# A new order of the steps of both mixing stages, its buffer table, and VectorE or GpSimd for 29 more instructions a layer

## The chip, the cores and the metric

The kernel runs on one core of a Trainium2 chip, as one launch. The metric is the device time of that launch in microseconds (us). Three runs of the kernel before took 1262.16, 1263.69 and 1265.23 us, the median being 1263.69.

The engines are named as in the profile: PE is TensorE (matrix products into PSUM), DVE is VectorE, ACT is ScalarE, POOL is GpSimd, and SP is the queue that issues the DMAs. Each engine works through a queue of its own in order; an instruction that waits for another engine holds up all that stands behind it in its queue.

## The reference

Two layers of a hybrid decoder trunk for 512 positions of width 1024: a mixing stage of three kinds of heads side by side, and an MLP with a squared ReLU, then a last norm. All in float32.

```python
for l in range(DEPTH):                              # DEPTH = 2
    h = rms_norm(x, norm_mix_g[l])
    proj = h @ w_in[l]                              # 1024 -> 3*384 + 3*256 + 1408
    p_att, p_conv, p_rwkv = jnp.split(proj, [3 * ATT_W, 3 * ATT_W + 3 * CONV_W], axis=-1)
    q, k, v = jnp.split(p_att, 3, axis=-1)
    ...
    o_att = diff_attention(q, k, v, lam, subln_g[l], lambda_init)    # 6 heads, causal
    b_gate, c_gate, u = jnp.split(p_conv, 3, axis=-1)
    o_conv = short_conv(b_gate, c_gate, u, conv_w[l])                # 3 taps
    o_rwkv = rwkv7_time_mix(p_rwkv, ...)                             # 6 heads, a recurrence over the positions
    mixed = jnp.concatenate([o_att, o_conv, o_rwkv], axis=-1)
    x = x + mixed @ w_out[l]
    h = rms_norm(x, norm_mlp_g[l])
    x = x + jnp.square(jax.nn.relu(h @ w_mlp_up[l])) @ w_mlp_down[l]
return rms_norm(x, final_norm_g)
```

## The kernel before

**Tiling.** x is held transposed, as eight tiles x 0 to x 7 of 128 channels by 512 positions. A projection is cut into groups of 128 output columns. To keep float32 accuracy each operand is a sum of two parts, a rounded one and its rest: for the activations ahim and alom (written by ACT at L431 and by DVE at L432), for the weights whi (the cast, ACT, L679) and wlo (the rest raw - whi, L691, on DVE or POOL). A weight group comes in two halves of 128x512 (named 0 and 4 by their first input tile), into three buffers each for raw, whi and wlo. One group is 24 products of 128x512, three for each input tile (ahim with whi, alom with whi, ahim with wlo), all through the helper of line L296, into one PSUM bank pj. Its evacuation, a DVE operation that multiplies with the norm's reciprocal root rsm (pk, pg, pr at L804, kf at L1259, vf at L1286), frees the bank.

**The mixing stage.** It has 26 groups of input projection, the differential attention of three head pairs, the short convolution, RWKV-7 for three head pairs, 8 output groups in two cuts (po, added to x at L732), and the first three groups of the MLP's up-projection (up). While PE works through the products of the groups, the small work of the heads is put between them: Gram products pg of RWKV (L296, from ar and bk, which DVE and POOL make at L942 to L945 from kkn, bb and k), transposes pk, pb, pa (L301), the scores sc of the attention, the masked row maximum (L1318), the exponentials (ACT, L1325), the weighted difference pp of the two softmaxes (L1332), its transposes ptt (L301) with their copies pT (ACT, L1341). RWKV's 64x64 triangular inverse starts with a chain of small POOL operations (tt and xb, L1150 and L1152). The norms' sums of squares run over the tiles: accm (L447) before the mixing stage, accf (L761) before the MLP; ones products pssm and pssf add them up over the channels, and a power on POOL (L377) and broadcast products prb make the reciprocal root.

**The order.** Nothing in the mixing stage is scheduled by the framework. The work is a set of generators, one a kind (m the products of the groups, w the casts, x and y the rests on DVE and on POOL, d the loads, e and q the entry's two parts, R, r, A, B and so on the heads' work), and a string of letters a layer, ORDER, says which generator emits its next instruction:

```python
for run in order.split():
    for _ in range(int(run[1:] or 1)):
        if next(work[run[0]], True) is None:
```

So each engine's queue has the order of that string. A second table, SLOTS, says which buffer of a tag each new tile takes (PSUM banks among them); a tile waits for the readers of the buffer's last tile. LO has a letter for each weight half: x puts its rest on DVE, y on POOL. SIDE has 29 letters a layer, read by `side` for: seven of the sums accf, and the RWKV operations k2 (L934), bb (L938), bk (L943), plo (L1008), nm (L1136), ee (L1176) of three pairs, and two each of the convolution's cz and cy (L1240, L1247); before, all 29 are on POOL.

The MLP that follows (groups up and dn, through L296, L352 and L353) is scheduled by the framework, from the state in which the mixing stage leaves the engines and banks.

Of the kernel before, what the change touches and what calls it, by code (L numbers as in the profile page):

```python
# [49 lines left out]
SIDE = ("yyyyyyyyyyyyyyyyyyyyyyyyyyyyy",  # L50
        "yyyyyyyyyyyyyyyyyyyyyyyyyyyyy")
# [4 lines left out]
LO = ("xxyyxxxxyxxyxyxyxyxyyxxxxyyxyyxxxyxyxyyyxxyxyyxxxxxyxxyyyxxyxyyyxxyxxyxxyyx",  # L56
      "xyxyyxxxxxyxxxxxxxxxxyxxyyyyyyxxyxxxxyyyyyyyxxxxyxxyyxyxyyxxyyxyxyyxyxxxxx")

ORDER = (
# [58 lines left out]
SLOTS = (  # L118
         "cp/rk 010 "
         "cp/ro 010 "  # L120
         "cp/rr 01 "
         "cp/rsx 01201201 "
         "cp/ry 010 "
         "cp/ys 010 "
# [158 lines left out]
def tile_trunk(ctx: ExitStack, tc: tile.TileContext, xT, wts, prm_d, cst_d, lora_d, gup_d, lam_d, fin_d, out):  # L283
# [85 lines left out]
    def root_steps(y, x, n, pad, add=None):  # L369
# [8 lines left out]
        for _ in range(pad):  # L378
            yield True
# [1241 lines left out]
```

## Time and profile before

| | |
|---|---|
| runs, median | 1263.69 us |
| the profiled execution, its own time | 1263.21 us |
| its span, first to last instruction | 1261.3 us |
| granted PE clock, share of full speed | 0.998 |
| mixing stages (layer 0, layer 1), about | 0 to 305, 632 to 925 us |

The profile has one execution. Its page gives the busy time of each engine; the list of waits gives, for an engine and an operation, by what it was held up: microseconds in total, times, longest. In the timeline a row has start, duration, engine, line, operation, result and operands by name, and in brackets the idle time before it with the operation that ended it. Groups of instructions have count, then busy time and mean duration in ns, then the idle time before them.

### The profile page before, as it was taken

How to read it: one execution, taken by the hardware profiler on the slowest of the kernel's cores; microseconds unless marked ns; L12 is line 12 of the kernel's file. 1: busy time of each engine (PE TensorE's matmuls, PEld its weight loads, DVE VectorE, ACT ScalarE, POOL GpSimd, SP SyncE). 2: the span in 40 equal slices, each digit the busy share in tenths (PEclk: the TensorE clock that was granted, in tenths of full speed). 3: DMA queues.
4: the chain of work that ended last, by engine and by line, in shares of the span. 5: the costliest groups of instructions: out<-in, count | busy, mean ns of one | idle time of the engine just before them, and what ended most of it. 6: DMA issues, size and time to landing. Idle time of an engine off the chain costs nothing.

```text
span 1261.3 us, 25029 instructions
## 1 busy us (share of the span) xinstructions
PE 1240.0 (98%) x9493; PEld 1049.8 (83%) x9493; DVE 889.3 (71%) x1728; ACT 695.4 (55%) x1474; POOL 359.4 (28%) x464
## 2 busy tenths in 40 slices
PE   9999999999999999999999999999999999999997
PEld 6777878787789898989877787888887989898987
DVE  6787777857967676765667777778598666666654
ACT  6675755646745454544475656564565545454553
POOL 1344627243200101010224355453431011111110
PEclk9999999999999999999999999999999999999999
DMA  6523323142333332321235333331424333333122
GB/s 213 159 85 94 109 94 101 52 140 78 106 121 101 101 101 101 101 86 50 77 101 146 98 102 109 98 97 60 134 93 134 96 106 100 102 101 101 60 76 76
DMA packets 84696, 127.92 MB, mean 101 GB/s; under 512 B 21472, under 2 KB 25568, under 8 KB 84576
## 3 DMA queue, kind: packets, MB, share of 16 engines
q1 hardware_dynamic: 83856, 125.77, 31.4%
q8 instruction: 75, 1.23, 0.4%
q10 hardware_dynamic: 720, 0.55, 0.1%
q14 instruction: 45, 0.37, 0.1%
HBM read 117.11 MB, written 9.18 MB: 100 GB/s over the span
## 4 chain that ended last, share of the span: by engine, by line
PE 70%; DVE 4%; issue 2%; ACT 2%; POOL 0%; POOLq 0%; ACTq 0%; DVEq 0%
PE dn L296 22%; PE pj L296 11%; PE pa L296 11%; PE pb L296 6%; PE po L296 4%; PE up L296 4%; PE dnF L296 3%; PE pc L296 3%; PE sc L296 1%; DVE wlo L353 1%; PE ptt L301 1%; PE pg L296 1%; DVE blo L1455 0%; DVE x L1531 0%; PE pyy L296 0%
## 5 line engine op out<-in xcount | busy, mean ns | idle before, releaser
L1399 POOL TENSOR_TENSOR ml<-m,mh 128x512 fp32r<-128x512 f32 x64 | 93.4, 1461 | 506.3 <-ACT mh L1398 488.3
L352 ACT CAST whi<-raw 128x512 fp32r<-128x512 f32 x142 | 88.0, 620 | 174.0 <-PE dn L296 156.8
L296 PE MATMUL dn<-mh,whi 128*128 128x512 f32 x448 | 175.4, 391 | 2.2 <-DVE x L1531 2.2
L296 PE MATMUL dn<-ml,whi 128*128 128x512 f32 x448 | 174.7, 390 | 0.0
L296 PE MATMUL dn<-mh,wlo 128*128 128x512 f32 x448 | 174.7, 390 | 0.0
L296 PE MATMUL pj<-ahim,whi 128*128 128x512 f32 x392 | 157.7, 402 | 4.4 <-DVE vf L1286 1.7
L296 PE MATMUL pj<-ahim,wlo 128*128 128x512 f32 x392 | 158.3, 404 | 0.0
L296 PE MATMUL pj<-alom,whi 128*128 128x512 f32 x392 | 158.2, 403 | 0.0
L679 ACT CAST whi<-raw 128x512 fp32r<-128x512 f32 x142 | 87.7, 619 | 100.1 <-PE pj L296 41.4
L1531 DVE TENSOR_TENSOR x<-dn,x 128x512 f32<-128x512 f32 x112 | 76.9, 687 | 77.4 <-PE dn L296 77.4
L691 POOL TENSOR_TENSOR wlo<-raw,whi 128x512 fp32r<-128x512 f32 x62 | 81.3, 1311 | 166.1 <-ACT whi L679 153.0
L353 DVE TENSOR_TENSOR wlo<-raw,whi 128x512 fp32r<-128x512 f32 x142 | 115.3, 812 | 11.3 <-ACT whi L352 11.2
L1470 DVE TENSOR_TENSOR slo_p<-s,shi_p 128x512 fp32r<-128x512 f32 x96 | 70.9, 741 | 63.4 <-ACT shi_p L1469 60.8
L296 PEld LDWEIGHTS dn<-mh,whi 128*128 128x128 f32 x448 | 84.0, 188 | 21.8 <-ACT whi L352 2.6
L296 PEld LDWEIGHTS dn<-mh,wlo 128*128 128x128 f32 x448 | 84.1, 188 | 17.9
L296 PEld LDWEIGHTS dn<-ml,whi 128*128 128x128 f32 x448 | 84.1, 188 | 16.5
L296 PEld LDWEIGHTS pj<-ahim,whi 128*128 128x128 f32 x392 | 73.9, 188 | 19.8 <-issue 1.7
L1469 ACT CAST shi_p<-s 128x512 fp32r<-128x512 f32 x96 | 59.2, 618 | 49.7 <-PE pa L296 38.1
L296 PEld LDWEIGHTS pj<-ahim,wlo 128*128 128x128 f32 x392 | 73.8, 188 | 14.3 <-issue 0.9
L296 PEld LDWEIGHTS pj<-alom,whi 128*128 128x128 f32 x392 | 73.9, 188 | 14.0 <-issue 0.5
L296 PE MATMUL pa<-tlo,shi_p 128*128 128x256 f32 x288 | 81.4, 282 | 0.0
L296 PE MATMUL pa<-thi,shi_p 128*128 128x256 f32 x288 | 81.2, 282 | 0.0
(406 smaller groups left out, 3247.5 us busy)
## 6 DMA issues: line engine op xcount, KB each, us to landing
raw<-wts SPq DMA_DIRECT2D x389, 256.0 KB, 2.6
qs<-dqhi SPq DMA_DIRECT2D x24, 128.0 KB, 3.2
ks<-dkhi SPq DMA_DIRECT2D x24, 128.0 KB, 3.8
x<-xT SPq DMA_DIRECT2D x8, 256.0 KB, 4.5
dqhi<-qhi SPq DMA_DIRECT2D x6, 256.0 KB, 3.3
dqlo<-qlo SPq DMA_DIRECT2D x6, 256.0 KB, 3.1
dkhi<-khi SPq DMA_DIRECT2D x6, 256.0 KB, 2.6
dklo<-klo SPq DMA_DIRECT2D x6, 256.0 KB, 3.1
```

What stands on the lines that cost most here:

```text
L296: ins = nc.tensor.matmul(*a, **k)
L301: ins = nc.tensor.transpose(*a, **k)
L352: act.copy(hi[:, :n], raw[:, :n])
L353: (pool if a and lean[0] else dve).tensor_tensor(lo[:, :n], raw[:, :n], hi[:, :n].bitcast(F32), ALU.subtract)
L679: yield act.copy(hi[:, k0:k1], raw[:, k0:k1])
L691: yield eng.tensor_tensor(lo[:, k0:k1], raw[:, k0:k1], hi[:, k0:k1].bitcast(F32), ALU.subtract)
L1399: pool.tensor_tensor(lo, m, hi.bitcast(F32), ALU.subtract)
L1469: act.copy(hi, src)
L1470: dve.tensor_tensor(lo, src, hi.bitcast(F32), ALU.subtract)
L1531: dve.tensor_tensor(x[j], pt, x[j], ALU.add)
```

## The change

The four tables are written anew: ORDER and SLOTS of both layers, LO, and SIDE. `root_steps` loses its empty steps, which emitted nothing. The program has the same 11870 instructions as before and two more ACT_TABLE_LOAD. 39 weight rests go from DVE to POOL; 42 instructions go from POOL to DVE, 15 of them weight rests, 27 by SIDE (layer 0: accf 1, 3, 7, k2 of pair 2, bb of pair 0, all bk, all nm, cz 1, cy 0; layer 1: accf 1, 2, 3, 4, 5, 7, k2 of pair 0, bk of pairs 0 and 2, plo of pair 0, ee of pair 1, cz 0). On PE 1261 of 6780 rows move; of 577 pieces of small work between the groups' products 218 stand elsewhere, most by one or two products. Of SP's 537 transfers 42 move, by at most three places.

```diff
-SIDE = ("yyyyyyyyyyyyyyyyyyyyyyyyyyyyy",
-        "yyyyyyyyyyyyyyyyyyyyyyyyyyyyy")
+SIDE = ("xyxyyyxyyxxyyxxxyyyxxxyyyyxxy",
+        "xxxxxyxxyyyyyxyxxyyyyyyxyxyyy")
...
-LO = ("xxyyxxxxyxxyxyxyxyxyyxxxxyyxyyxxxyxyxyyyxxyxyyxxxxxyxxyyyxxyxyyyxxyxxyxxyyx",
-      "xyxyyxxxxxyxxxxxxxxxxyxxyyyyyyxxyxxxxyyyyyyyxxxxyxxyyxyxyyxxyyxyxyyxyxxxxx")
+LO = ("xxxxxxyxyxyyyxxxyyyyyxyxxyyyyyyyxxxxyyyyxyyyyxxyxxxyyyyyyyyyyxxxxyyxxxxxxy",
+      "xyxyyxxxyyxxyyxyxxyxyyxyyyyyyxxxyyyxyxyyyyyyyxxxxxyyyyyyyyyyxyxyxxxxyyxxyy")
 ORDER = (
-         "g d10 e w e m w x m w m x m2 x m q m2 w m x e m w e m x m w d m3 x d e m3 d2 e q m3 d e q m3 d q e d q d q d q w d w d x d w x d x d q m d "
...
-    def root_steps(y, x, n, pad, add=None):
+    def root_steps(y, x, n, add=None):
...
         yield pool.tensor_tensor(y, xx, mhalf.to_broadcast([P, n]), ALU.pow)
-        for _ in range(pad):
-            yield True
-
```

What the strings do is seen in the queues. Rows give the source line, which is 14 to 17 less after the change, the operation, result and operands (the number behind the last underscore counts tiles), and the shape.

DVE near the start of layer 0, at 10 to 17 us, before:

```order
L432 SCALAR_TENSOR_TENSOR alom0_3_191<-x3_72,prm0_66,ahim0_3_190 128x512
L447 TENSOR_TENSOR accm0_149<-accm0_149,sqm0_2_198 128x512
L447 TENSOR_TENSOR accm0_149<-accm0_149,sqm0_3_204 128x512
L691 TENSOR_TENSOR wlo24_s_111<-raw24_4_166,whi24_s_110 128x512
L691 TENSOR_TENSOR wlo18_s_113<-raw18_4_172,whi18_s_112 128x512
L691 TENSOR_TENSOR wlo15_s_115<-raw15_4_180,whi15_s_114 128x512
L447 TENSOR_TENSOR accm0_149<-accm0_149,sqm0_4_222 128x512
L432 SCALAR_TENSOR_TENSOR alom0_4_229<-x4_73,prm0_66,ahim0_4_228 128x512
L432 SCALAR_TENSOR_TENSOR alom0_5_241<-x5_74,prm0_66,ahim0_5_240 128x512
```

and after:

```order
L430 TENSOR_TENSOR accm0_149<-accm0_149,sqm0_2_195 128x512
L430 TENSOR_TENSOR accm0_149<-accm0_149,sqm0_3_201 128x512
L415 SCALAR_TENSOR_TENSOR alom0_3_199<-x3_72,prm0_66,ahim0_3_198 128x512
L674 TENSOR_TENSOR wlo24_s_111<-raw24_4_170,whi24_s_110 128x512
L674 TENSOR_TENSOR wlo18_s_113<-raw18_4_172,whi18_s_112 128x512
L415 SCALAR_TENSOR_TENSOR alom0_4_227<-x4_73,prm0_66,ahim0_4_226 128x512
L430 TENSOR_TENSOR accm0_149<-accm0_149,sqm0_4_230 128x512
L674 TENSOR_TENSOR wlo15_s_115<-raw15_4_180,whi15_s_114 128x512
L415 SCALAR_TENSOR_TENSOR alom0_5_241<-x5_74,prm0_66,ahim0_5_240 128x512
```

alom 3 went behind two sums; alom 4 went ahead of a sum and of the rest of group 15. On ACT ahim 4 went ahead of the square sqm 4 in the same way, and on PE the sum product pssm went seven products back.

ACT in layer 0 at 47 to 57 us (L926 and L927 the exponentials of the decay, L850 the sigmoid of the pair's a), before:

```order
L926 ACT_TABLE_LOAD
L926 ACTIVATE dx0_0_573<-lw0_0_451 128x8x64
L927 ACTIVATE di0_0_574<-lw0_0_451 128x512
L679 CAST whi25_4_605<-raw25_4_514 128x512
L932 ACTIVATE t10_0_609<-av0_0_499,drv0_101,prm0_66 128x512
L936 ACTIVATE kkn0_0_621<-zk0_0_465,prm0_66 128x512
L679 CAST whi1_0_629<-raw1_0_562 128x512
L1292 COPY v0_0_637<-pvt0_0_638 128x512
L1325 ACTIVATE pp0_0_0_0_0_674,s0q0_0_650<-pp0_0_0_0_0_674,mx0_0_0_0_0_675 128x128
```

and after:

```order
L909 ACT_TABLE_LOAD
L909 ACTIVATE dx0_0_571<-lw0_0_448 128x8x64
L662 CAST whi25_0_576<-raw25_0_477 128x512
L910 ACTIVATE di0_0_572<-lw0_0_448 128x512
L915 ACTIVATE t10_0_600<-av0_0_499,drv0_101,prm0_66 128x512
L662 CAST whi25_4_602<-raw25_4_514 128x512
L919 ACTIVATE kkn0_0_612<-zk0_0_467,prm0_66 128x512
L833 ACT_TABLE_LOAD
L833 ACTIVATE av0_2_627<-pa0_2_624,prm0_66 128x512
L662 CAST whi1_0_634<-raw1_0_540 128x512
L1275 COPY v0_0_638<-pvt0_0_639 128x512
L1308 ACT_TABLE_LOAD
```

The sigmoid av0_2, which stood with those of the other pairs, now stands between the exponentials, and two table loads come with it. Its products pa0_2 on PE moved with it, from the first groups to the end of group 6. On DVE at this place bb, ar, vf and bk of pair 0 now follow each other, where bb and bk were on POOL.

PE at the end of input group 20 in layer 0, at 129 to 132 us, before:

```order
L301 MATMUL pb_0_1_1790<-cst_77,bk0_1_1634 128x128 x4
L296 MATMUL pj0_20_1694<-ahim0_5_240,wlo20_4_1581 128x512
L296 MATMUL pj0_20_1694<-ahim0_6_252,whi20_4_1575 128x512
L296 MATMUL pj0_20_1694<-alom0_6_253,whi20_4_1575 128x512
L296 MATMUL pj0_20_1694<-ahim0_6_252,wlo20_4_1581 128x512
L296 MATMUL pj0_20_1694<-ahim0_7_261,whi20_4_1575 128x512
L301 MATMUL pa_0_1_1811<-cst_77,ar0_1_1633 128x128 x4
L296 MATMUL pj0_20_1694<-alom0_7_262,whi20_4_1575 128x512
L296 MATMUL pj0_20_1694<-ahim0_7_261,wlo20_4_1581 128x512
L296 MATMUL sc0_1_0_0_0_1829<-ks0_1_0_1383,qs0_1_0_1348 128x128
L296 MATMUL sc0_1_0_0_1_1831<-ks0_1_0_1383,qs0_1_0_1348 128x128
L296 MATMUL pj0_17_1842<-ahim0_0_130,whi17_0_1656 128x512
```

and after:

```order
L282 MATMUL pj0_20_1721<-ahim0_6_252,wlo20_4_1578 128x512
L282 MATMUL pj0_20_1721<-ahim0_7_269,whi20_4_1576 128x512
L282 MATMUL pj0_20_1721<-alom0_7_270,whi20_4_1576 128x512
L282 MATMUL pj0_20_1721<-ahim0_7_269,wlo20_4_1578 128x512
L282 MATMUL sc0_1_0_0_0_1811<-ks0_1_0_1383,qs0_1_0_1346 128x128
L282 MATMUL sc0_1_0_0_1_1813<-ks0_1_0_1383,qs0_1_0_1346 128x128
L287 MATMUL pb_0_1_1817<-cst_77,bk0_1_1637 128x128 x4
L287 MATMUL pa_0_1_1835<-cst_77,ar0_1_1636 128x128 x4
L282 MATMUL pj0_17_1844<-ahim0_0_130,whi17_0_1687 128x512
```

The transposes pb and pa went from inside the group to behind its last product, between the group and the next one; the bank of group 17 still waits for the evacuation of group 20 (pk, DVE). At 682 us in layer 1 pk, pb and pa move in the same way, and at 122 us the second half of the Gram products pg of pair 1 goes ahead of the transposes of vf and of group 20's first product, while the rest wlo17_0, which stood ahead of vf on DVE, goes to POOL. At 86 us the rest wlo4_0 goes from DVE to POOL, and at 807 us pp goes ahead of the second half of the sum ysum on DVE.

In the MLP the framework's order of two groups is exchanged. Before, in layer 0 twelve products of up-group 4 stand ahead of group 3, and in layer 1 group 3 stands whole ahead of group 4; after, it is the other way round. At the start of layer 1 DVE takes x 7 right after x 6, ahead of the rest of the first group's weights, and the cast whi of these weights stands behind one more entry tile and takes a buffer that the last down-projection group reads.

More of the change, by code (lines that the diff above doesn't have):

```diff
@@ L120 @@
          "cp/ro 010 "
-         "cp/rr 01 "
+         "cp/rr 10 "
          "cp/rsx 01201201 "
@@ L132 @@
          "mp/dc 010 "
-         "mp/ks 101010 "
+         "mp/ks 010101 "
          "mp/lw 012 "
@@ L139 @@
          "mp/pp 011001100110011001100110011001100110011001100110 "
-         "mp/qs 101010 "
+         "mp/qs 010101 "
          "mp/s0q 010 "
@@ L144 @@
          "mp/tc 010110 "
-         "mp/tp 01234510245234513512041025023524520013000341351302 "
+         "mp/tp 01234510245245414312051023042345340012002051031024 "
          "mp/tq 010101010101 "
          "mp/ty 010101010 "
-         "ps/at 010101010101010101010101010101010101010101010101010101010101010101010101010101010101 "
+         "ps/at 101010101010101010101010101010101010101010101010101010101010101010101010101010101010 "
          "ps/mm 01011101010001010101010101010101010101010 "
-         "ps/rp 01233303103102310231023102310231023102021301230123012032121023102310202130123012301230123012013201313021032 "
-         "wp/raw 01201201201201201201201201201201201201201201201201201201201201201201201201 "
-         "wp/sq 010100001010101 "
+         "ps/rp 01233303103210321031230123012301230123231021302130213203131203102310202130123012301230123012301230101320312 "
+         "wp/raw 01201201210210210210210210210210210210210210210210210210210210210210210210 "
+         "wp/sq 101011010101010 "
          "wp/whi 01201201201201201201201201201201201201201201201201201201201201201201 "
@@ L180 @@
          "mp/tc 010100 "
-         "mp/tp 01234510245235423143150241324125123504132413453420 "
+         "mp/tp 01234510245325432412450314231435432501423124154130 "
          "mp/tq 010101010101 "
@@ L184 @@
          "ps/at 010101010101010101010101010101010101010101010101010101010101010101010101010101010101 "
-         "ps/mm 01010100101010101010110101010101010101010101 "
-         "ps/rp 01230123012301230123012301231023102021301230123012301230123021032121302310231023013201320123012323102130 "
-         "wp/raw 01201201201201201201201201201201201201201201201201201201201201201201201201 "
-         "wp/sq 010101010 "
-         "wp/whi 01201201201201201201201201201201201201201201201201201201201201201201201201 "
-         "wp/wlo 01201201201201201201201201201201201201201201201201201201201201201201201201 ")
+         "ps/mm 10101011010101010101001010101010101010101010 "
+         "ps/rp 10321032103210321023102310231023102021301230123012301230130231203131023012302130120312031203210303120132 "
+         "wp/raw 12012012012012010210210210210210210210210210210210210210210210210210210210 "
+         "wp/sq 101010101 "
+         "wp/whi 21021021021021021021021021021021021021021021021021021021021021021021021021 "
+         "wp/wlo 21021021021021020120120120120120120120120120120120120120120120120120120120 ")
 NG = NG_IN + NG_OUT + NG_UP + NG_DN
@@ L770, in inner_norm @@
                 r = cp.tile([P, NB], F32, tag="rr", bufs=2, name=f"rr{key}")
-                yield from root_steps(r, pt[:, :NB], NB, 4)
+                yield from root_steps(r, pt[:, :NB], NB)
                 rb = psum("rp", 4, f"prb{key}")
@@ L788, in norm @@
                 r = cp.tile([P, NB], F32, tag="rr", bufs=2, name=f"rr{key}")
-                yield from root_steps(r, pt[:, :NB], NB, 4)
+                yield from root_steps(r, pt[:, :NB], NB)
                 yield from got(ready, "ex")
@@ L1115, in rwkv_pair @@
                 ry = cp.tile([P, 2 * NB], F32, tag="ry", bufs=2, name=f"ry{n}")
-                yield from root_steps(ry, st_, 2 * NB, 10, add=gn_eps.to_broadcast([P, 2 * NB]))
+                yield from root_steps(ry, st_, 2 * NB, add=gn_eps.to_broadcast([P, 2 * NB]))
                 y8 = ysum.rearrange("p b h f -> p (b h) f")
@@ L1355, in att_pair @@
                 ro = cp.tile([P, 2 * NB], F32, tag="ro", bufs=2, name=f"ro{n}")
-                yield from root_steps(ro, oss, 2 * NB, 11, add=s0q)
+                yield from root_steps(ro, oss, 2 * NB, add=s0q)
                 o8 = ot.rearrange("p b (h f) -> p (b h) f", f=HD)
```

99 rows, old and new, of the table ORDER are left out of this document.

## The prediction

> **What bounds the kernel now.** I read three views, in this order: the busy times, the list of what TensorE (PE) waits for, and the timeline at those waits.
>
> ```profile
> PE 1240.0 (98%) x9493; PEld 1049.8 (83%) x9493; DVE 889.3 (71%) x1728; ACT 695.4 (55%) x1474; POOL 359.4 (28%) x464
> ...
> PE pj L296 <- DVE vf L1286: 1.7, 2, 0.9
> PE ptt L301 <- DVE pp L1332: 1.3, 2, 0.8
> PE pj L296 <- DVE pg L804: 1.1, 1, 1.1
> PE pssm L296 <- DVE accm L447: 0.9, 1, 0.9
> PE up L296 <- DVE wlo L353: 0.8, 1, 0.8
> PE pj L296 <- DVE pk L804: 0.7, 1, 0.7
> PE pssm L296 <- DVE drv L461: 0.7, 1, 0.7
> PE pj L296 <- ACT ahim L431: 0.7, 1, 0.7
> PE up L296 <- ACT whi L352: 0.5, 1, 0.5
> PE pj L296 <- DVE kf L1259: 0.4, 1, 0.4
> PE pj L296 <- DVE alom L432: 0.4, 1, 0.4
> ...
> PE up L296 <- DVE bn L1432: 0.2, 1, 0.2
> ```
>
> PE is busy throughout, so the number of products sets the time, and the change alters none of them. The twelve waits quoted (total, times, longest) sum to 9.4 us: all that a better order can win where the order is written by hand, up to the first rows of the MLP. The other half of the span is untouched.
>
> What a wait costs is a little more than its idle time. Here is one, at 86 us.
>
> ```profile
> 83.38 1.29 POOL L1176 TENSOR_TENSOR ee<-nn,cst 128x512 f32<-128x512 f32 x1
> 83.53 1.68 DVE L691 TENSOR_TENSOR wlo<-raw,whi 128x512 fp32r<-128x512 f32 x1
> ...
> 84.55 0.39 PE L296 MATMUL pj<-ahim,wlo 128*128 128x512 f32 x1
> 84.77 0.39 PE L296 MATMUL pj<-ahim,whi 128*128 128x512 f32 x1
> ...
> 85.99 0.33 PE L301 MATMUL ptt<-cst,pp 128*128 128x128 f32 x1 [0.83 <-DVE pp L1332]
> ```
>
> Products start every 0.23 us (84.55, 84.77) though each is shown 0.39 long. From 84.77 to 85.99 are 1.22, so the wait costs 0.99: its idle 0.83 plus 0.16. I add 0.15 for each of the fourteen occurrences in the list, so the ceiling is about 11.5 us.
>
> **The change part by part.** The page speaks of one execution of 1263.21 us (span 1261.3); the sum is made against it, and the median of the three runs, 1263.69, lies 0.5 higher.
>
> **The start, 14 to 21 us.**
>
> ```profile
> 14.00 0.63 ACT L444 ACTIVATE sqm<-x 128x512 f32<-128x512 f32 x1
> ...
> 14.54 1.51 ACT L431 ACTIVATE ahim<-x,prm 128x512 fp32r<-128x512 f32 x2
> ...
> 15.30 0.50 PE L296 MATMUL pj<-ahim,whi_s 128*128 128x512 f32 x1 [0.70 <-ACT ahim L431]
> ...
> 16.18 0.50 PE L296 MATMUL pj<-alom,whi_s 128*128 128x512 f32 x1 [0.39 <-DVE alom L432]
> ```
>
> The first ahim of the pair at 14.54 runs behind the square (sqm, 0.63). The change puts ahim 4 ahead of it and alom 4 ahead of the sum accm and of a weight rest: both come some 0.6 earlier, which wins 0.6 of the 1.24 lost there. pssm, the norm's sum, moves seven products (1.6 us) back, past its wait of 0.7: another 0.85. Together 1.5 (bounds 0.6 and 2.1).
>
> **46 to 66 us.**
>
> ```profile
> 53.68 1.78 POOL L938 TENSOR_TENSOR bb<-kkn,av 128x512 f32<-128x512 f32 x1
> ...
> 53.87 0.48 PE L296 MATMUL pj<-ahim,whi 128*128 128x512 f32 x1 [0.88 <-DVE vf L1286]
> ...
> 54.23 1.78 DVE L942 SCALAR_TENSOR_TENSOR ar<-kkn,dx 128x512 f32<-128x512 f32 x1
> ```
>
> bb and bk go to DVE, where they run ahead of vf or just behind it. vf comes about 0.6 later, while pa 2 (0.45 of products) now stands in front of this wait. The Gram products pg move twelve products forward, onto DVE's new bk: up to 0.5 of wait. In return DVE evacuates pg, the gate's group, ahead of kq, and the wait of 1.1 later on goes. I take a gain of 0.5 (bounds: a loss of 1.5, if both loads below bind, and a gain of 1.4).
>
> **Two more table loads** stand on ACT there, since the sigmoid av 2 now lies between the exponentials.
>
> ```profile
> 54.81 0.59 ACT L1292 COPY v<-pvt 128x512 f32<-128x512 f32 x1 [1.35 <-PE pvt L301]
> 56.26 0.40 ACT L1325 ACTIVATE pp<-pp,mx 128x128 f32<-128x128 f32 x1 [0.85 <-DVE mx L1318]
> ...
> 88.35 1.28 ACT L860 ACT_TABLE_LOAD   x1
> 89.64 0.63 ACT L860 ACTIVATE zg<-zg 128x512 f32<-128x512 f32 x1
> ```
>
> 2 x 1.28 is 2.6 us, plus the sigmoid. ACT waits 1.35 and 0.85 for others there, which takes up most of it; the first softmax slips by some 0.6 with the sigmoid. Its consumer ptt doesn't wait today (the two waits on pp in the list are at 86 and 807 us), products of the group pj stand ahead of it, and I count 0; with that cover gone the 0.6 would be paid, and the whole 2.6 if the holes close too. The Trainium skill (ScalarE: Activation LUTs, "What ACT_TABLE_LOAD costs") puts a switch at 2.66 us, a load and a drain of 1.38. By that the two would take 5.3 us, the softmax would slip by over 3 and the sum come out some 2 us higher, near 1261. The rows here have no room for such a drain: the activation follows 0.01 us after the load.
>
> **Four waits that the new order covers.**
>
> ```profile
> 120.64 0.69 DVE L691 TENSOR_TENSOR wlo<-raw,whi 128x512 fp32r<-128x512 f32 x1
> ...
> 121.36 0.69 DVE L1286 TENSOR_TENSOR vf<-pj,rsm 128x512 f32<-128x512 f32 x1
> ...
> 122.20 0.47 PE L296 MATMUL pj<-ahim,whi 128*128 128x512 f32 x1 [0.79 <-DVE vf L1286]
> ...
> 130.97 0.69 DVE L1001 COPY ab<-pa 128x512 f32<-128x512 f32 x1 [0.40 <-PE pa L301]
> ...
> 131.58 0.68 DVE L804 TENSOR_TENSOR pk<-pj,rsm 128x512 f32<-128x512 f32 x1
> ...
> 132.31 0.50 PE L296 MATMUL pj<-ahim,whi 128*128 128x512 f32 x1 [0.75 <-DVE pk L804]
> ```
>
> At 122 the rest in front of vf goes to POOL, and the second half of the Gram products (1.0 us) comes ahead of the wait: won 0.95. At 132 the transposes pb and pa leave the group and fill the time while DVE evacuates it, and pk goes ahead of the copy ab: won 0.85. At 682 pk, pb and pa do the same for kf: won 0.5. At 86 the rest that took 1.68 beside POOL's ee goes to POOL: won 0.9. Together 3.2 (bounds 1.6, if half of them return elsewhere, and 3.5).
>
> At 807 DVE takes pp ahead of the second half of ysum (0.43) and ptt stays where it is: won 0.5. At 632, where layer 1 begins, DVE now takes x 7 straight after x 6; the bank of the first group passes to x 7, and the cast of its weights waits for the last down-projection. PE starts about 0.6 later, but the squares' sum, which stops it 0.9 at 637, comes earlier: won 0.2 (bounds: a loss of 1, a gain of 0.7).
>
> **The first MLP groups.**
>
> ```profile
> 305.95 0.50 PE L296 MATMUL up<-ahif,whi 128*128 128x512 f32 x1 [0.53 <-ACT whi L352]
> ...
> 307.54 0.50 PE L296 MATMUL up<-ahif,wlo 128*128 128x512 f32 x1 [0.85 <-DVE wlo L353]
> ```
>
> Group 4 runs ahead of group 3 in layer 0, on weights that aren't there yet: 0.53 + 0.85, the 0.2 on bn in the list, and 3 x 0.15 make 2.0 lost. Layer 1 has them in order and no such wait. The change exchanges the layers: 3 before 4 in layer 0, 4 before 3 in layer 1. So layer 0 wins 2.0 and layer 1 loses as much: 0 (bounds minus 1.5, plus 1.5, since the rows of layer 1 differ).
>
> **81 instructions change engine.** A rest costs 1.31 on POOL and 0.72 on DVE:
>
> ```profile
> L691 POOL TENSOR_TENSOR wlo<-raw,whi 128x512 fp32r<-128x512 f32 x62 | 81.3, 1311 | 166.1 <-ACT whi L679 153.0 <-PE pj L296 7.7 <-DVE mlo L872 2.7
> L691 DVE TENSOR_TENSOR wlo<-raw,whi 128x512 fp32r<-128x512 f32 x37 | 26.8, 724 | 3.1 <-ACT whi L679 2.9
> ```
>
> 39 rests go to POOL, 42 instructions to DVE: DVE changes by about 42 x 0.7 - 39 x 0.72 = +1 us, POOL by 51 - 55 = -4. Neither engine is the bound, and most rests have whole groups of products ahead of their first use: 0, hidden behind those products. If POOL's queue, where the inverse's small operations also stand, makes one late, PE pays the lateness.
>
> **The rest.** Of 577 pieces of small work between the big products 218 change place; about 160 of these lie outside the places named. At the old list's rate (9.4 us over 577) they would bring 2.6 us of fresh waits; with none, 0. I take 1.5. Bunching the small pieces I count as nothing: they fill the same slots (the 0.23 us rhythm goes on on both sides of them).
>
> Sum: -1.5 - 0.5 - 3.2 - 0.5 - 0.2 + 0 + 1.5 = -4.4, so 1258.8 for that execution and 1259.3 against the median. I say 1259.
>
> **The rivals.**
>
> *Nothing to be seen.* The waits quoted belong to DVE, ACT and PE in turn; a PE that arrives earlier may meet the next operand late. If half of the 5.9 gained returns and the fresh waits are 2.6, the change is -0.3: 1263.4. For it: at the start the wait on alom follows that on ahim within 1 us (15.30, 16.18). Against it: at 122 and 132 the time is filled with work that is ready.
>
> *Slower: weights late behind POOL.* POOL runs the inverse as a serial chain in the same stretch in which 39 more rests enter its queue, each 1.31 instead of 0.72, and the cast and the reload of the buffer follow each. The rows that speak for it are the 1.68 at 83.53 and 1.78 at 54.23: DVE beside POOL takes 1.0 longer. If ten of the 39 come 1.0 late, that is +10, and +5.6 in all: 1269. From about seven such pieces on (2.5 + 4.4) the change is slower by over 0.2%. Against it: POOL is 28% busy.
>
> *Much faster.* All of the 11.5 goes, nothing fresh comes, and only layer 1's exchange brings 2.0 and its slack 0.5 back: -9, 1254.7. Against it: searches leave residues, and the old order still has its fourteen.
>
> *The table loads bind*: the holes close because DVE and PE come earlier, the softmax starts up to 2.6 late, and about 2 of it reaches PE through its pair's chain: 1261. The row at 88.35 speaks for the price, the holes against it. By the switch cost that the Trainium skill gives (ScalarE: Activation LUTs, the same section) this would be the likelier case.
>
> **How the numbers follow.** Forecast 0.40 (own range 1256 to 1261), table loads 0.08, nothing 0.20, slower 0.22, much faster 0.10. A measurement of this kernel tells 0.2% (2.5 us) from no change, so faster is below 1261.2 and slower above 1266.2. Faster: the forecast, much faster and half of the table case, 0.54; same: 0.24 with the other half; slower: 0.22. The range 1254 to 1268 takes in the forecast, the same case and the near half of the slower one, and leaves out what lies beyond ten late weights.
>
> **What would show it.** In the profile after: no PE wait on ahim near 15 us above 0.3 and none on drv; no wait on vf at 122, on pk at 132, on pp at 86 or kf at 682; a wait on whi and wlo of the MLP at 926 in layer 1 and none at 306; two table loads between 52 and 57 us with ptt not waiting behind them. Wrong would be: PE waits on a POOL wlo in several places, each near 1 us, or a list of PE waits as long as before with other names.

## The result: 8.8 us faster, and the profile after

| | us | range of runs |
|---|---|---|
| before, median of 4 runs | 1263.51 | 1262.16 to 1265.23 |
| after, median of 4 runs | 1254.74 | 1253.71 to 1255.20 |
| profiled execution before: time, span | 1263.21, 1261.3 | |
| profiled execution after: time, span | 1255.07, 1253.1 | |

The ratio is 0.9929, interval 0.9912 to 0.9946. The forecast was 1259. The time lies in the range given (1254 to 1268), 0.7 above its foot and below the forecast's own (1256 to 1261), and on the number of the rival "much faster", though for another reason.

The busy times of the page after:

```profile
PE 1233.6 (98%) x9493; PEld 1055.0 (84%) x9493; DVE 903.3 (72%) x1731; ACT 697.5 (56%) x1476; POOL 358.2 (29%) x461
```

The list of PE's waits after, without those at the program's two ends and without four of 0.2 to 0.3:

```profile
PE pssm L282 <- DVE accm L430: 1.6, 1, 1.6
PE ptt L287 <- DVE pp L1315: 1.4, 2, 1.2
...
PE dn L282 <- DVE x L1514: 1.2, 3, 0.7
...
PE pj L282 <- DVE x L1514: 0.9, 1, 0.9
PE up L282 <- DVE wlo L339: 0.9, 1, 0.9
...
PE pj L282 <- DVE alom L415: 0.8, 2, 0.5
PE pot L287 <- DVE ot L1341: 0.8, 1, 0.8
PE px L282 <- DVE yi L1161: 0.5, 1, 0.5
PE up L282 <- ACT whi L338: 0.5, 1, 0.5
PE up L282 <- DVE bn L1415: 0.4, 1, 0.4
PE pvt L287 <- DVE vf L1269: 0.3, 1, 0.3
```

And in the timeline after, the two waits on pp:

```profile
87.02 0.44 PE L287 MATMUL ptt<-cst,pp 128*128 128x128 f32 x2 [0.19 <-DVE pp L1315]
...
764.88 0.55 PE L287 MATMUL ptt<-cst,pp 128*128 128x128 f32 x3 [1.20 <-DVE pp L1315]
```

The list has other names and is hardly shorter: its rows, those at the two ends included, sum to 14.9 us before and 13.3 after. What fell is PE's *busy* time, from 1240.0 to 1233.6, with the same 9493 products. That is 6.4 of the 8.2 us by which the span fell. A busy time that falls without fewer products means that the products cost less.

To see where, I took the time from each PE start to the next and set against it the usual pitch of that kind of product (0.227 for 128x512), the same in every kernel. What goes beyond it is called a wait if it is large (over 0.15, at a change of tile 0.25 to 0.30) and PE stands idle in it, throttled if it is as large without idle time, and a small excess otherwise. Other limits move a few tenths of a us from one column to the next. In us, from one profiled execution each:

```
kernel              start to start   waits   throttled   small excess
before                      1254.1    18.5         3.2           79.6
after                       1245.9    17.4         3.6           72.2
new_first_layer             1244.9    13.4         3.9           74.9
new_second_layer            1255.6    21.1         4.5           77.2
pieces_apart                1253.1    19.1         4.4           76.8
products_behind             1249.7    17.7         7.0           72.2
engines_as_before           1252.9    21.8         6.0           72.4
boundary                    1244.4    15.9         3.9           71.8
up_in_order                 1245.1    16.9         3.6           71.9
before_bunched              1266.6    27.6         5.3           80.9
after_bunched               1251.6    23.3         3.6           72.0
mixed_bunched               1254.3    21.7         3.4           76.5
```

From before to after the waits fall by 1.1 and the small excess by 7.4. Most of that stands where PE goes from the big products to small pieces and back. Entries from a big product to a small piece fell from 281 to 207, as the pieces now stand in bunches. By the change that PE makes between two starts (two changes make a round trip), count and small excess in us:

```
changes of tile                               before        after
to a tile narrower than 128, or from it       128  16.6     112  14.0
between two such tiles                        170   2.9     176   3.5
to or from the scores' 96 rows                159   6.3     129   2.2
between other full-width pieces               291  -3.1     250  -3.8
between pieces of one shape                  8744  56.8    8825  56.3
```

### The profile page after: what moved, and what is told of

Its sections match the earlier page's. It is cut to its first block, busy times and chain, and to the rows that moved or that the text cites. A ratio compares the mean times of both kernels' runs of the same rounds, so it can differ in the third digit from the quotient of the medians.

```text
span 1253.1 us, 25011 instructions
## 1 busy us (share of the span) xinstructions
PE 1233.6 (98%) x9493; PEld 1055.0 (84%) x9493; DVE 903.3 (72%) x1731; ACT 697.5 (56%) x1476; POOL 358.2 (29%) x461
## 5 line engine op out<-in xcount | busy, mean ns | idle before, releaser
L674 POOL TENSOR_TENSOR wlo<-raw,whi 128x512 fp32r<-128x512 f32 x84 | 110.5, 1316 | 189.2 <-ACT whi L662 159.4
```

Source lines behind the costliest of these rows:

```text
L674: yield eng.tensor_tensor(lo[:, k0:k1], raw[:, k0:k1], hi[:, k0:k1].bitcast(F32), ALU.subtract)
```

## Experiments

### Which layer

One layer has all four tables of the change, the other those of the kernel before (with its empty steps in `root_steps` for that layer only).

> Order, buffers and both choices of engine of the change in the first layer, all of the kernel before in the second. By the landmarks of the two traces the first layer with its MLP is 8.25 us earlier at 318 us and the second adds nothing net: 1255.3. By the prediction's terms (start 1.5, 46 to 66 0.5, 86, 122 and 132 2.7, MLP groups 2.0, half of the fresh waits lost 0.75): -5.95, 1257.5. Rival (the gain sits in the second layer): 1261 or more.

> The tables of the kernel before in the first layer, those of the change in the second. By the landmarks: boundary +1.5, mixing -2.9, MLP groups +2.6, so about +1: 1264 to 1265. By the prediction's terms (632 0.2, 682 0.5, 807 0.5 won, MLP groups 2.0 and fresh waits 0.75 lost): +1.55, 1265.

Measured: the new first layer alone 1254.36 (0.9927, 0.9914 to 0.9939), the new second alone 1263.87 (0.9999, 0.9991 to 1.0008). So the whole gain sits in the first layer, as the landmarks, the starts of the same stages in the two traces, had it; by the prediction's own terms the first layer would have come to 1257.5. The small excess adds up: -4.7 and -2.4 are -7.1, where the whole change has -7.4. The waits do so less well: -5.1 and +2.6 are -2.5, where the whole change has -1.1. In the second layer the new order wins 2.4 of small excess and loses as much in waits.

### Setting the bunches apart again, and a control

In `pieces_apart` 93 products that stood just ahead of a bunch of small pieces go between the pieces. In `products_behind`, the control, 53 of them go behind the bunch. The first place in the string where they differ:

```diff
-m4 w m2 g m g4 y R m3
+m4 w m2 g3 m g2 y R m3      pieces_apart, next place
+m4 w m2 g4 m g y R m3       products_behind
```

> The changed kernel with 93 neighbouring pairs of small steps of TensorE set apart by one product each, which stood just ahead of the bunch; all other engines keep their order. Switches from the products to small pieces in the two hand-ordered stretches: 184 to 277. Theory of switches: 93 x 0.087 (6.4 us of TensorE busy time by 74 switches fewer) = +8 us, 1263, up to +16 if most pairs are of the dear kind; the busy time of TensorE grows by as much. Rival (the gain came from the waits removed, and bunching is free): within 2 us of 1254.7, busy time of TensorE within 1 us of 1233.6, and whatever is lost stands in its list of waits.

> The control: the changed kernel with 53 products that stood just ahead of a bunch of small steps put just behind the whole bunch, so that the number of switches stays 184. Theory of switches: 1254.7 within 1.5 us, busy time of TensorE within 1 us of 1233.6. Rival (any product moved in a tuned order costs, by a wait or a late operand): 53/93 of what setting the pieces apart costs, some +4.5 us.

Measured: apart 1263.66 (0.9998, 0.9989 to 1.0006), all of the gain gone; the control 1256.46 (0.9946, 0.9934 to 0.9957). Small excess +4.6 apart and 0.0 in the control, waits +1.7 and +0.3. Busy time of PE is 1240.5 apart, that of the kernel before. The theory of switches holds in its direction and in the control. Its price was too high: 4.6 over 93 switches are 0.05 each, not the 0.087 expected, and a third of the 7.2 lost in the profiled execution is waits and the throttle, so that 1263 was met partly by luck.

The control misses what was expected of it by a little: its median lies 1.7 above the change, not within 1.5, and its busy time is 1237.4 instead of within 1 of 1233.6. Its profiled execution took 1258.92, and 3.4 of that, against the change, is throttle: in two stretches of 3.4 us the granted clock (PEclk, third from the end) was half.

```profile
core 0: us, PE busy (x) PEld busy (x) DVE busy (x) ACT busy (x) POOL busy (x), PEclk, DMA share, GB/s
...
630.60:634.00 3.40, 3.40 (x11) 2.75 (x10) 0.00 (x0) 0.62 (x1) 1.44 (x2) 0.50 0.44 163
...
709.10:712.50 3.40, 3.40 (x33) 2.78 (x37) 0.97 (x6) 1.74 (x7) 0.19 (x1) 0.50 0.00 0
```

The four executions of the control whose mean clock was 0.996 or more took 1255.0 to 1256.6.

### What a switch costs

`probe` puts small pieces among the 12 products of each down-projection group:

```diff
+                            pe.matmul(pt, w, a, start=(n == 0), stop=(n == 11))
+                            n += 1
+                            extra(tail, w.bitcast(F32), a.bitcast(F32), 2 * l + h % 2,
+                                  ({}, {6: 2}, {4: 2, 8: 2}, {6: 4})[j % 4].get(n, 0))
```

> The changed kernel with extra small pieces among the 12 products of each down-projection group of the MLP, written to a bank that nobody reads: none in columns 0 and 4, one bunch of two in 1 and 5, two bunches of two in 2 and 6, one bunch of four in 3 and 7. The pieces are fp32: 64x64 in the even eighths of layer 0, transposes of 128x128 in its odd ones, 32x32 in the even eighths of layer 1, 96 rows by 128 in its odd ones. Read from the trace: the length of a group from its first to its last product. Theory of switches: two bunches of two are longer than one bunch of four by 0.15 to 0.25 us for 64x64 and 32x32, by under 0.05 for the transposes, by 0.05 to 0.15 for 96 rows. Rival (a small piece costs its slot, wherever it stands): the same length to 0.03 us for all four. The time as a whole says nothing here.

> The same probe with eight other kinds of piece, by eighth of the MLP (columns 0 and 4 none, 1 and 5 one bunch of two, 2 and 6 two bunches of two, 3 and 7 one bunch of four). Layer 0: eighths 0 and 4 a tile of 128 rows by 64 columns, 1 and 5 of 64 by 128, 2 and 6 a product of 128x128 (no transpose), 3 and 7 of 64x64, all fp32. Layer 1: 0 and 4 64x64 in the upper quadrant, 1 and 5 64x64 alternating between the lower and the upper one, both fp32, 2 32x32 in fp32r, 3 64x64 in fp32r. If the size of the tile makes a switch dear: every kind that is narrower than 128 in rows or columns costs 0.25 to 0.35 us for the second bunch, fp32r or not, and the 128x128 product under 0.05. Rival (the type does it, fp32 among fp32r products): the fp32r kinds under 0.05, the 128x128 product in fp32 0.25 to 0.35.

The timeline of PE in `probe`, two neighbouring groups of layer 0. The first has two bunches of two 64x64 pieces, the second one bunch of four; an fp32 piece leaves two records:

```profile
333.02 0.39 PE L282 MATMUL dn<-mh,whi 128*128 128x512 f32 x1
333.33 0.44 PE L282 MATMUL pq<-mh,whi 64*64 64x64 f32 x4
333.71 0.51 PE L282 MATMUL dn<-ml,whi 128*128 128x512 f32 x1
334.05 0.40 PE L282 MATMUL dn<-mh,wlo 128*128 128x512 f32 x1
...
337.39 0.39 PE L282 MATMUL dn<-mh,wlo 128*128 128x512 f32 x1
337.71 0.68 PE L282 MATMUL pq<-mh,wlo 64*64 64x64 f32 x8
338.32 0.50 PE L282 MATMUL dn<-mh,whi 128*128 128x512 f32 x1
```

The same with two transposes of 128x128, in the next eighth:

```profile
369.77 0.39 PE L282 MATMUL dn<-mh,whi 128*128 128x512 f32 x1
370.00 0.38 PE L287 MATMUL pq<-cst,mh 128*128 128x128 f32 x2
370.13 0.48 PE L282 MATMUL dn<-ml,whi 128*128 128x512 f32 x1
```

The product ahead of the 64x64 pieces holds its slot 0.31 instead of 0.23, and the one behind them 0.34; nothing is marked as idle. Ahead of a transpose the slot is 0.23. Median length of a group from first to last product, and its difference, which is the price of one more round trip:

```
piece (rows x columns of the tile)         two bunches of 2   one of 4   round trip
64x64 fp32                                       3.68            3.35       0.33
  the same in the upper quadrant                 3.68            3.35       0.33
  alternating lower, upper                       3.44            3.10       0.34
  128 columns moving                             4.08            3.76       0.32
64x64 fp32r                                      3.40            3.06       0.34
32x32 fp32                                       3.40            3.10       0.30
32x32 fp32r                                      3.27            2.95       0.31
128x64 fp32                                      3.67            3.33       0.34
64x128 fp32                                      4.11            3.78       0.33
96 rows by 128, fp32                             3.46            3.41       0.05
128x128 product, fp32                            3.41            3.40       0.01
128x128 transpose                                2.99            2.97       0.01
```

So every tile tried that has 64 or 32 rows or columns costs 0.30 to 0.34 a round trip, whatever its type. A tile of 96 or 128 rows by 128 columns costs nearly nothing. The rival of the type falls. The price for narrow tiles lies above the 0.15 to 0.25 that I expected, that of 96 rows at the foot of its range.

The Trainium skill (TensorEngine Tiling (Array Packing), "Key Properties") says that a change of tiling mode, though not of the tile within one, drains TensorE. The probes agree: pieces that alternate between two tiles of one size pay no more for a round trip (0.34) than pieces that stay in one.

Applied to the two kernels, with half the changes of the table above as round trips: 8 fewer to narrow tiles are -2.6 (measured -2.6, and +0.6 among narrow tiles), 20 fewer among other full-width pieces -0.2 (measured -0.7), 15 fewer to the scores -0.7 (measured -4.1). Between pieces of one shape 0.5 went without a price. Applied to `pieces_apart`: 9 more to narrow tiles +3.0 (measured +3.4), 22 to the scores +1.1 (measured +1.5).

So the scores fell by 3.4 more than the price. In the kernel before, 31 of 71 scores behind a product start over 0.28 after it, where most of the others take 0.23; after, 7 of 51. A stretch of the kernel before shows two reasons:

```profile
704.53 0.50 PE L301 MATMUL ptt<-cst,pp 128*128 128x128 f32 x3
...
704.78 0.48 PE L296 MATMUL pj<-alom,whi 128*128 128x512 f32 x1
...
705.11 0.40 PE L296 MATMUL sc<-ks,qs 96*128 96x512 f32 x1
...
705.34 0.39 PE L296 MATMUL pj<-ahim,wlo 128*128 128x512 f32 x1
705.60 0.19 PEld L296 LDWEIGHTS sc<-ks,qs 96*128 96x128 f32 x1 [0.30 <-ACT pT L1341]
705.60 0.50 PE L296 MATMUL sc<-ks,qs 96*128 96x512 f32 x1
...
705.93 0.39 PE L296 MATMUL pj<-ahim,whi 128*128 128x512 f32 x1
```

The first score, at 705.11, starts 0.33 after its product, but that product started only 0.03 after the last of the three transposes (at 704.75), where transposes follow each other every 0.11. Both steps together take 0.345, by their usual pitches 0.336. Of the 31 late scores 24 stand so, one product behind a transpose, and a product in that place starts as late (0.314). After the change 6 stand so. These 18 fewer, at some 0.085 each, took 1.5 from the row of the scores in the table, and that is no saving: time only passed to other rows.

The second score, at 705.60, is a wait that PE's list doesn't show. PEld loads the weights of the products, and its own list has, before and after:

```profile
PEld sc L296 <- ACT pT L1341: 4.3, 16, 0.4
...
PEld sc L282 <- ACT pT L1324: 0.5, 2, 0.3
```

The scores and the transposes ptt take turns in the two banks of one tag (`at`), so a score waits for the copy pT that empties a bank. All 16 such scores of the old order stand one product behind the score before: the copy isn't done, the weights come late, and the score (0.26) and the product behind it (0.33) both start late. They cost, with the slot behind them, 2.1 us more than their pitches, the two after the change 0.3: 1.8 won. Without these two parts 0.8 of the 4.1 is left, which the price covers. Of the whole -7.4, the prices give 3.5 (2.6, 0.2 and 0.7), these waits 1.8, and 0.6 is lost among narrow tiles; some 2.7 have no place.

### The engines undone

```diff
-SIDE = ("xyxyyyxyyxxyyxxxyyyxxxyyyyxxy",
-        "xxxxxyxxyyyyyxyxxyyyyyyxyxyyy")
+SIDE = ("yyyyyyyyyyyyyyyyyyyyyyyyyyyyy",
+        "yyyyyyyyyyyyyyyyyyyyyyyyyyyyy")
```

> The changed kernel with its order and buffers, but the 29 selectable instructions of each layer all back on GpSimd; the choice for the weight rests stays as changed. Prediction's step (engine changes are hidden): 1254.7 within 1.5 us. Rival (the choice of engine carries the gain, since the order was written for it): +3 to +9 us, with waits on GpSimd results in TensorE's list.

Measured: 1261.65 (0.9987, 0.9978 to 0.9996), 6.9 above the change, as the rival said. By SIDE 25 instructions change engine (POOL has 486 here and 461 in the change), not the 27 named in the section on the change. The small excess is unchanged (+0.2), waits +4.4, throttle +2.4. The throttle is two stretches of 3.4 us at half the clock, at 57.2 and 770.6, and each follows one of the two longest waits: 1.91 on bk, and 2.40 on pp at 770, where the change waits 1.20. The first of them, in the timeline of that kernel:

```profile
54.37 1.26 POOL L926 TENSOR_TENSOR bk<-bb,di 128x512 f32<-128x512 f32 x1
...
55.68 1.25 PE L282 MATMUL pg<-ar,bk 64*64 64x128 f32 x48 [1.91 <-POOL bk L926]
```

and the same place in the changed kernel, where DVE makes bk:

```profile
50.32 1.28 ACT L833 ACT_TABLE_LOAD   x1
...
52.55 0.68 DVE L926 TENSOR_TENSOR bk<-bb,di 128x512 f32<-128x512 f32 x1
52.69 0.66 PE L287 MATMUL pvt<-cst,vf 128*128 128x128 f32 x4 [0.33 <-DVE vf L1269]
...
54.10 1.28 ACT L1308 ACT_TABLE_LOAD   x1
54.26 1.25 PE L282 MATMUL pg<-ar,bk 64*64 64x128 f32 x48
55.79 0.40 ACT L1308 ACTIVATE pp<-pp,mx 128x128 f32<-128x128 f32 x1 [0.41 <-DVE mx L1301]
```

In the new order the choice of engine is what lets pg stand twelve products earlier without a wait. What it would bring in the old order was not run.

### The boundary and the exchanged groups

The timeline of the changed kernel at the boundary, then the first MLP groups of layer 1:

```profile
623.64 0.62 ACT L662 CAST whi<-raw 128x512 fp32r<-128x512 f32 x1 [1.63 <-issue]
...
624.72 0.47 PE L282 MATMUL pj<-ahim,whi 128*128 128x512 f32 x1 [0.94 <-DVE x L1514]
...
628.67 1.27 POOL L674 TENSOR_TENSOR wlo<-raw,whi 128x512 fp32r<-128x512 f32 x1 [0.17 <-ACT whi L662]
628.74 1.75 DVE L430 TENSOR_TENSOR accm<-accm,sqm 128x512 f32<-128x512 f32 x1
630.54 1.05 PE L282 MATMUL pssm<-ones,accm 128*128 128x1 f32 x8 [1.60 <-DVE accm L430]
...
916.53 0.50 PE L282 MATMUL up<-ahif,whi 128*128 128x512 f32 x1 [0.53 <-ACT whi L338]
...
918.14 0.50 PE L282 MATMUL up<-ahif,wlo 128*128 128x512 f32 x1 [0.88 <-DVE wlo L339]
...
921.09 0.47 PE L282 MATMUL up<-ahif,whi 128*128 128x512 f32 x1 [0.38 <-DVE bn L1415]
```

```diff
-         "ps/mm 10101011010101010101001010101010101010101010 "
+         "ps/mm 01010100101010101010110101010101010101010101 "
...
-         "wp/whi 21021021021021021021021021021021021021021021021021021021021021021021021021 "
+         "wp/whi 01201201201201201201201201201201201201201201201201201201201201201201201201 "
```

with wp/wlo renumbered likewise (`boundary`); and, alone, the last digits of the second layer's ps/rp from 0132 to 0123 (`up_in_order`).

> The changed kernel with the second layer's tables for the projections' PSUM banks (ps/mm) and the two weight tiles (wp/whi, wp/wlo) renumbered: the first group takes the bank and the buffers that have been free longest, as in the kernel before; all else as changed. If the boundary at 625 to 632 loses 1.5 by these two numbers: -1.5, 1253.2, and the wait on x 7 there gone. Rival (the norm's sum, which waits for the last addition of squares, sets it whatever the first group does): within 0.7 of 1254.7, the wait on the sum that much longer.

> The changed kernel with the last two entries of the second layer's table of PSUM buffers (ps/rp) exchanged, so that MLP group 3 gets the bank that comes free first and runs ahead of group 4, as in the first layer. If group 4 ahead of its weights costs what the trace shows (0.68 + 1.05 + 0.54 at 917 to 921): -2.3, 1252.4. Rival (group 3 or the next group meets the same late weights): within 0.7 of 1254.7.

Measured: the boundary 1253.74 (0.9920, 0.9907 to 0.9934), 1.0 below the change, waits -1.5 in the profile; the intervals of the two overlap, and the time lies between the two expectations, so the runs do not decide. In its timeline both waits are shorter:

```profile
624.25 0.47 PE L282 MATMUL pj<-ahim,whi 128*128 128x512 f32 x1 [0.31 <-DVE x L1514]
...
629.27 1.05 PE L282 MATMUL pssm<-ones,accm 128*128 128x1 f32 x8 [0.85 <-DVE accm L430]
```

The groups in order took 1254.92 (0.9932, 0.9918 to 0.9945): nothing won, where I expected 2.3. The three waits at 917 to 921 are gone and PE is 2.8 us ahead of the changed kernel at group 5, but two waits come later in its timeline:

```profile
949.58 0.47 PE L282 MATMUL dn<-mh,whi 128*128 128x512 f32 x1 [1.15 <-DVE x L1514]
...
1017.55 0.39 PE L282 MATMUL pa<-thi,shi_p 128*128 128x256 f32 x1 [0.49 <-DVE c L1498]
```

In the changed kernel neither stands: PE comes late enough.

### Bunching alone

If a switch costs, products between two pieces should be put ahead of both. Here that is done by a simple rule, for both kernels and for the mixed one:

```diff
-m w m2 g2 m g2 x m g2
+m w m2 g m g3 x m g2        before_bunched, layer 0, first place
```

> The kernel before, with nothing changed but products that stood between two small steps of TensorE put ahead of both, where no weight, load or new group lies between; all other engines keep their order, engines and buffers stay. Switches in the hand-ordered stretches: 258 to 213, among them 20 round trips to the scores' 96-row tiles and 2 to narrower ones. Theory of switches: 45 times 0.05 to 0.096 us (what a switch came to in the kernel with pieces apart, and between the two kernels), so -2.2 to -4.3: 1259.4 to 1261.5, TensorE's time outside waits down by as much. Rival (bunching gains only together with the new order): 1263.7 within 1.

> The changed kernel with the renumbered tables at the boundary and the same bunching: switches 184 to 165. Boundary -1.0 as measured, 19 switches -0.9 to -1.8: 1252.3 within 0.8. Rival (what is left doesn't bunch for free: the products put ahead make the small steps late): 1253.7 or more.

> First layer of the change, second of the kernel before, both bunched: switches 217 to 188. From 1254.4 by 29 switches: -1.5 to -2.8, 1252.3 within 0.8. Rival: as for the other.

All three missed, to the other side: 1275.18 (1.0088, 1.0074 to 1.0102), 1261.51 (0.9979, 0.9970 to 0.9988) and 1262.83 (0.9990, 0.9981 to 0.9998). Against their bases the waits rise by 9.1, 7.4 and 8.3, and the small excess does not fall (+1.3, +0.2, +1.6). The first row of the list of waits of `before_bunched`:

```profile
PE pst L294 <- DVE st L1076: 2.4, 6, 0.4
```

and the first place of it in its timeline:

```profile
112.08 0.33 PE L294 MATMUL pst<-db,ad 128*128 128x64 f32 x2
112.52 0.28 DVE L1076 SCALAR_TENSOR_TENSOR st<-pst,dc,db 128x64 f32<-128x64 f32 x1 [0.71 <-PE pst L294]
112.86 0.43 PE L294 MATMUL pst<-st,ad 128*128 128x64 f32 x2 [0.45 <-DVE st L1076]
```

pst and st are the steps of the recurrence: each pst needs the st made from the pst before it, some 0.8 later. The products between them were not spare; they hid that. In `before_bunched` waits of pst grew by 4.1, those of the scores by 2.0, those of pzw, which takes the inverse, by 1.4. In `after_bunched` the scores' wait for pT, told above, stands in PE's own list with 1.4. The rule put such dependent steps side by side, and 43 of the 45 round trips that it removed from the kernel before lead to tiles of 128 columns, the scores' among them, which the probes find nearly free. No version that was run beats the change by more than its interval.

## Why the prediction was right, and where it was wrong

**Where the time went.** "Bunching the small pieces I count as nothing: they fill the same slots (the 0.23 us rhythm goes on on both sides of them)" is the step that failed. The only small piece among the prediction's rows is a transpose, and beside a transpose the rhythm does go on (369.77, 370.00). Beside 64x64, 32x32 and 128x64 tiles a round trip costs 0.33. The term is -7.4 instead of 0: 3.5 by prices that the probes measured, 1.8 by waits of weight loads for pT, less 0.6 among narrow tiles; 2.7 have no mechanism. The 9.4 us of waits were also not "all that a better order can win": PEld's list had 4.3 more, on the scores.

**The waits.** Their sum was put at -4.4 and is -1.1. The direction and nearly all places were right, the size was not. First layer: terms of -5.95, measured -5.1. Second layer: terms of +1.55, measured +2.6. The sums of the two layers are also not quite those of the whole change (-2.5 against -1.1). So the forecast came near by luck: the waits gave 3.3 less than forecast, and the term put at 0 gave 7.4 more. The -4.4 was not confirmed.

**The four covered waits** (3.2): confirmed place by place. No wait on vf at 122, on pk at 132 or on kf at 682 is left; that on pp at 86 is 0.19 instead of 0.83.

**The start** (1.5): the waits on ahim and on drv are gone as said, but alom took part of it back (0.8 in the list, 0.4 before). By the starts of the same products of the groups PE was 0.4 to 1.1 ahead between 36 and 50 us, not 1.5.

**46 to 66** (0.5): the wait of 1.1 on pg's evacuation is gone, vf keeps 0.33 at 52.69, and pg waits for nothing. By the same products the gain was about 1.6, larger than the term. The two more table loads bind nothing: they stand at 50.32 and 54.10, ACT then waits 0.80 for PE and 0.41 for DVE, and no ptt waits behind them. No drain shows either: the load at 54.10 begins 0.02 after the copy before it ended. The rival of the table loads falls.

**807** (0.5): the wait is gone, but one of 1.2 on pp came at 765, which is what the term for fresh waits was for.

**632** (0.2 won): a loss of about 1.5. I saw that the cast waits and that the bank passes to x 7, and priced it at 0.6; the sum pssm, which I had put earlier, waits 1.60 instead of 0.86, as the last accm takes 1.75 beside POOL's rest, where it took 0.68 before.

**The MLP groups** (exchange, 0): the waits went over to layer 1 exactly as read, 0.53, 0.88 and 0.38 for 0.53, 0.85 and 0.2. But the two layers do not cancel. By the starts of the same products layer 0 won 2.35 at these groups and kept it to its end; layer 1 lost 2.63 and had 1.66 of it back by 979, where the kernel before waits 0.97 for x at 959 and the changed one, coming later, does not. So the exchange was worth about 1.4, not 0.

**The engines** (0, "hidden behind those products"): undone under the new order they cost 4.4 of waits, so they are not independent of the order; under the old one they were not run. DVE's busy time rose by 14.0, where the prediction had about 1, and POOL's fell by 1.2, where it had 4.

**The rivals.** "Much faster" had the number, 1254.7, and the wrong cause: it needed all waits to go, and 17.4 are left. "Weights late behind POOL" is not seen: PE's list has no wait on a POOL rest.

## What to carry to other kernels

When busy time falls or rises at the same number of products, look at the pitch at each change of tile: between full 128x512 products and tiles of 64 or 32 rows or columns, count round trips and price each at about 0.33 us. Group such narrow pieces where they do not depend on each other, and leave products between those that do: full-width pieces may stand singly. Read the waits of the weight loads (PEld) beside those of the products: a late load lengthens two slots without an idle row on PE. A wait read in the trace is worth its idle time only if the next engine in line has no wait of its own to put in its place; run the removal alone before it enters a sum.

## What the hardware showed unexpectedly

- A round trip from 128x512 products to a 64x64, 32x32, 128x64 or 64x128 tile and back took 0.30 to 0.34 us, without idle time in the profile; to 96 or 128 rows by 128 columns 0.01 to 0.05.
- In a bunch, a 64x64 piece took 0.131 us in one quadrant and 0.062 when the pieces alternated between two (from bunches of two and of four, 2.976 and 3.100 against 3.089 and 3.352). The Trainium skill (TensorEngine Tiling (Array Packing), "Key Properties") says that different tiles can load and multiply in parallel; these lengths agree.
- In five of the profiled executions the granted clock fell to 0.50 for 3.4 us at a time inside the program, seven times in all, which is 1.7 us of lost clock each. Six of the seven came within 2.2 us of an idle time of PE of 0.65 to 2.40; the wait of 1.60 at 630.54 in the changed kernel was followed by none. A long wait can so cost more than its idle time.
